# Sums on VectorE, whole quarter loads and a written order for three engines in two lead-ins of a decoder layer

## The chip, the cores and the metric

The kernel runs on one core of a Trainium2 chip. Its time is the device time of one execution in microseconds (us). The engines are named as in the profile: PE is TensorE (PEld its weight loads), DVE is VectorE, ACT is ScalarE, POOL is GpSimd, SP is SyncE, which issues the DMAs here.

## The reference

One decoder layer on 1024 tokens of width 1024, all in float32: token mixing (stick-breaking attention beside a state-space mixer), cross-attention to 256 memory tokens, and a SwiGLU feed-forward of hidden width 2816. Each of the three is normalised before and after and added to the stream.

```python
h = rms_norm(x, g_pre_mix[l])
...
x = x + rms_norm(merged @ w_mix_out[l], g_post_mix[l])
h = rms_norm(x, g_pre_xa[l])
mem_n = rms_norm(mem, g_mem[l])
x = x + rms_norm(memory_cross_attention(h, mem_n, w_xq[l], w_xkv[l], w_xo[l]), g_post_xa[l])
h = rms_norm(x, g_pre_ffn[l])
x = x + rms_norm(swiglu(h, w_gu[l], w_down[l]), g_post_ffn[l])
```

The two places that the change touches are `h @ w_xq`, the first product of the cross-attention, and the first four blocks of `h @ w_gu`, the first product of the feed-forward.

## The kernel before

A product of float32 matrices is made of three matmuls on the high and low parts of its operands: high by high, high by low, low by high. The high part of a weight is rounded by ScalarE (`hi_sb`, L98), the low part is the difference, made by VectorE or GpSimd (`lo_of`, L101). `acc3` (L216 to L223) makes one product of a 512-row weight block of 128 columns with 512 tokens, 12 matmuls of 128x512, into one PSUM bank.

The two projections go by a scheme of Strassen's kind on 2x2 blocks. The activation `h` has the blocks b11, b21, b22 and the combinations t1 to t4, each kept as a high and a low tile; of a weight come the quarters q11, q12, q21, q22, and from them s1 = q21 + q22, s2 = s1 - q11, s3 = q11 - q21, s4 = q12 - s2. Seven products make a pair of output rows (p = 0 and 1, since a quarter holds two column blocks).

A lead-in is the stretch in which such a projection begins while the output projection before it ends. `out_proj` (L1431 to L1458) works through the last four chunks of 128 tokens; each chunk is normalised (`pre_norm`, L159 to L172: ScalarE's square, two small GpSimd operations for the root, VectorE's scaling on L163), then transposed by TensorE and spread by `put` (L1497 to L1510: two copies on ScalarE, six 128x512 operations on VectorE). The list `late` holds the transposes and the put of the chunk that is still to be done. Products that need only the first half of the tokens (b11, b21) are made while the last chunks are on their way: `lead_products` makes three of them from weights that were split ahead; n0, n1 (of quarter n11), q1 (of q12) and n2, n3 (of n12) come next. n11, n12, n21, n22 are the quarters of the second pair of output rows. `first_sum` (L1577) adds two products: ScalarE copies the one out of PSUM (L1578), VectorE adds the other (L1579). `other_products` (L1581 to L1623) then does t1, t2, t3, b22 and t4 for one pair; it runs twice, the first time also splitting the blocks t2 to t4 (`other_blocks`). The sums s1 to s4 are made by GpSimd (`combined`, L1587).

The order of the products on TensorE is written out by hand: `in_turn` (L1563) holds each product behind the one before it. The other engines' order is the scheduler's, but for a few places held by `behind`. In the query projection the raw quarters q21, q22 and q12 lie in free halves of the result tiles `qT`, two halves of two tiles each (`parted`), so each is loaded by two DMAs of 256 KB; n11 and n12 lie whole in qT6 and qT7, and q11, n21, n22 in buffers of the pool `t4`. In PSUM the query lead-in has two single banks (`bank`) and two tiles of two banks each (`two_banks`); the feed-forward gives the pool of the two-bank tiles back after its first sums and opens `psf`, six single banks.

Of the kernel before, what the change touches and what calls it, by code (L numbers as in the profile page):

```python
# [16 lines left out]
P = 128  # L17
# [15 lines left out]

@with_exitstack
def hybrid_block(ctx, tc, a, out, dbg=None):
    nc = tc.nc
    V, A, G, T = nc.vector, nc.scalar, nc.gpsimd, nc.tensor
# [51 lines left out]
    def hi_sb(o, i, eng=None):  # L89
        if eng is None:  # L90
            turn[0] += 1
            eng = "pa"[turn[0] % 2]
        if eng == "p":
            return G.tensor_scalar(o, i, 1.0, 0.0, ALU.mult, ALU.add)  # L94
        elif eng == "v":
            return V.tensor_copy(o, i)
        else:
            return A.activation(o, i, AF.Copy)  # L98

    def lo_of(o, i, hi, eng=V):  # L100
        return eng.tensor_tensor(o, i, hi.bitcast(F32), ALU.subtract)  # L101
# [48 lines left out]
    rstd_ops = []  # L150

    def rstd_of(ms):
        r = mk(stats, [P, 1], F32, "rstd")
        G.tensor_scalar(r, ms, EPS, None, ALU.add)  # L154
        rstd_ops.append(G.tensor_tensor(r, r, mhalf, ALU.pow))
# [3 lines left out]
    def pre_norm(psp, xt, yt, gbc, put):  # L159
# [5 lines left out]
        def turns():  # L165
# [5 lines left out]
            put(pts, yt)  # L171
# [1262 lines left out]
    def out_proj(half, act, w, t4, psp, x_src, x_dst, gpost, gpre, put, ahead=None):  # L1434

        wh, wl = w
        for ci in range(4):
# [19 lines left out]
            if late:  # L1457
                late.pop()()  # L1458
# [68 lines left out]
    def quarter(t):  # L1527

        v = t.rearrange("p (k b f) -> p k b f", k=4, b=2)
        return [(v.rearrange("p k b f -> p k (b f)"), 0, 2 * P)], [v[:, :, p] for p in range(2)]  # L1530

    def parted(h0, h1):

        v = [h.rearrange("p (k f) -> p k f", k=4) for h in (h0, h1)]
        return [(x, p * P, P) for p, x in enumerate(v)], v

    def quarter_load(q, w, kh, c0):
        for dst, o, n in q[0]:
            ins = nc.sync.dma_start(dst, w[kh * 512:(kh + 1) * 512, c0 + o:c0 + o + n].rearrange("(k p) f -> p k f", p=P))
        return ins  # L1540

    split_ops = []

    def split_weight(pl, tag, x, eng=V):
        o = mk(pl, [P, 2, 4, P], F32R, tag)
        split_ops.append([hi_sb(o[:, 0], x, "a"), lo_of(o[:, 1], x, o[:, 0], eng)])
        return o[:, 0], o[:, 1]

    def lead_weights(wbig, w):
# [4 lines left out]
        ws = {(0, p): split_weight(ld, "sw", raws[0][:, :, p]) for p in range(2)}  # L1554
        o = mk(wbig, [P, 2, 4, P], F32R, "wraw", 2)
        hi_sb(o[:, 0], raws[1][:, :, 0], "a")
        lo_of(o[:, 1], raws[1][:, :, 0], o[:, 0])
        ws[1, 0] = o[:, 0], o[:, 1]
        return ws

    chain = []

    def in_turn(ps, w, b, first, last):  # L1563

        with behind(chain[-1:]):
            chain.append(acc3(ps, w, b, first, last))
        return chain[-1]

    def first_product(hb, w, nm, ps):
        return in_turn(ps, w, hb[nm], True, nm == "b21")  # L1570

    def lead_products(hb, ws, pa, pb0):
        first_product(hb, ws[0, 0], "b11", pa[0])
        first_product(hb, ws[0, 1], "b11", pa[1])
        first_product(hb, ws[1, 0], "b21", pb0)

    def first_sum(y, pa, pb):  # L1577
        A.activation(y, pa, AF.Copy)  # L1578
        V.tensor_tensor(y, y, pb, ALU.add)  # L1579

    def other_products(hb, pa, pc, q11, q12, q21, q22, sfp, swp, y, last, blocks=None):  # L1581

        a11, a12, a21, a22 = [q[1] for q in (q11, q12, q21, q22)]

        def combined(dst, x, z, op):
            for o, i, j in zip(dst, x, z):
                G.tensor_tensor(o, i, j, op)  # L1587
            return dst

        def rooms():  # L1590
            return [mk(sfp, [P, 4, P], F32, "sf") for _ in range(2)]
# [3 lines left out]

        def products(ps, ws, nm, start, stop, then):
            for p in range(2):
                in_turn(ps[p], ws[p], hb[nm], start, stop)
# [538 lines left out]
```

## Time and profile before

| | us |
|---|---|
| median of 3 runs | 2564.26 (2561.57 to 2564.91) |
| the profiled execution | 2562.7 |
| its span, first to last instruction | 2561.0 |
| PE busy | 2460.5 |
| DVE busy | 1818.6 |
| ACT busy | 1164.5 |
| POOL busy | 884.7 |

The mean granted TensorE clock is 0.992 of full speed. In the rows of the profile, "L1579" is the line of the kernel, "qT<-qT,p" says what is written from what, "x2" how many instructions the row holds, and the bracket at its end how long the engine was idle before it and what ended that. The query lead-in lies from about 1634 to 1735 us of the span, the one of the feed-forward from about 1897 to 1987.

### The profile page before, as it was taken

Reading aid. Unit: us, or ns where it says so; the run is one execution under the profiler, and the core shown is the slowest. Engines: PE = TensorE matmul, PEld = TensorE weight load, DVE = VectorE, ACT = ScalarE, POOL = GpSimd, SP = SyncE. Lnnn points to the kernel's source line nnn. Section 1 sums busy time; section 2 is a strip of 40 time slices with the busy share of each in tenths; the row PEclk is TensorE's granted clock in tenths of the full one; section 3 lists DMA queues with packets and bytes.
Section 4 is the critical chain, followed back from the end, with each engine's and each line's share of the span. In section 5 each row is a group of like instructions: output and inputs, shape, how many; then the busy total and the mean of one; then the engine's idle time right before and its main releaser. Section 6 shows DMA issues by size and latency. Waiting matters only on the chain. (4 is left out here: it accounts for less than half of the span.)

```text
span 2561.0 us, 33402 instructions
## 1 busy us (share of the span) xinstructions
PE 2460.5 (96%) x12306; PEld 2017.4 (79%) x12306; DVE 1818.6 (71%) x2131; ACT 1164.5 (45%) x2075; POOL 884.7 (35%) x672
## 2 busy tenths in 40 slices
PE   7999999999999999999999999889999999999998
PEld 5788888888788788777777778767777888888876
DVE  7765877766678787698898654745467566665997
ACT  5333555555566655566554203424334333334343
POOL 3221644443112111256665131311133233323662
PEclk9999999999999999999999999999999999999999
DMA  7441443333443443365342642401241222234232
GB/s 246 152 127 57 137 135 103 108 111 112 123 111 101 114 110 93 109 202 162 99 118 79 227 155 74 149 32 50 92 139 62 91 87 74 83 96 167 99 132 99
DMA packets 250718, 295.63 MB, mean 115 GB/s; under 512 B 17071, under 2 KB 170680, under 8 KB 250426
## 3 DMA queue, kind: packets, MB, share of 16 engines
q1 hardware_dynamic: 249978, 291.40, 36.4%
q8 instruction: 97, 1.59, 0.3%
q10 hardware_dynamic: 576, 2.10, 0.2%
q14 instruction: 67, 0.55, 0.1%
HBM read 202.20 MB, written 74.45 MB: 108 GB/s over the span
## 5 line engine op out<-in xcount | busy, mean ns | idle before, releaser
L903 DVE TENSOR_TENSOR_SCAN n<-n,mask 128x128 f32<-128x128 f32 (+7 forms) x128 | 187.7, 1491 | 24.6 <-ACT n L902 23.3
L101 DVE TENSOR_TENSOR sw<-sf,sw 128x512 fp32r<-128x512 f32 x166 | 137.3, 837 | 91.0 <-ACT sw L98 88.8
L98 ACT ACTIVATE sw<-sf 128x512 fp32r<-128x512 f32 x166 | 102.6, 627 | 136.3 <-PE mm L222 112.2
L920 ACT ACTIVATE wth<-tr,mone 128x512 fp32r<-128x512 f32 x192 | 110.6, 585 | 81.1 <-PE tr L917 79.1
L220 PE MATMUL mm<-h,sw 128*128 128x512 f32 x368 | 143.3, 389 | 2.6 <-ACT t L1615 2.6
L221 PE MATMUL mm<-h,sw 128*128 128x512 f32 x368 | 143.2, 389 | 0.0
L222 PE MATMUL mm<-h,sw 128*128 128x512 f32 x368 | 140.9, 389 | 0.0
L921 DVE SCALAR_TENSOR_TENSOR wtl<-tr,wth 128x512 fp32r<-128x512 f32 x192 | 99.5, 543 | 48.2 <-ACT wth L920 48.2
L101 DVE TENSOR_TENSOR sw<-wr,sw 128x512 fp32r<-128x512 f32 x113 | 107.1, 949 | 35.3 <-ACT sw L98 35.2
L98 ACT ACTIVATE sw<-wr 128x512 fp32r<-128x512 f32 x114 | 71.8, 630 | 111.6 <-PE mm L222 109.1
L188 POOL TENSOR_TENSOR sf<-wr,wr 128x512 f32<-128x512 f32 x36 | 51.0, 1416 | 205.3 <-DMA wr<-in_w_gu_dram 140.6
L685 DVE SCALAR_TENSOR_TENSOR b<-b,prmT,b 128x1023 f32<-128x1023 f32 (+2 forms) x72 | 109.5, 1521 | 16.9 <-ACT b L679 16.4
L94 POOL TENSOR_SCALAR v<-va 128x512 fp32r<-128x512 f32 x16 | 20.6, 1287 | 283.4 <-PE av L930 164.4
L154 POOL TENSOR_SCALAR rstd<-ms 128x1 f32<-128x1 f32 x74 | 29.4, 397 | 242.4 <-ACT x L1450 112.6
L902 ACT ACTIVATE n<-sc 128x512 f32<-128x512 f32 (+1 forms) x192 | 88.7, 494 | 46.7 <-PE tr L917 28.8
L104 PE MATMUL mm<-oth,bw 128*128 128x512 f32 x256 | 103.7, 405 | 3.2 <-DVE a L1242 3.2
L104 PE MATMUL p<-bw,h 128*128 128x512 f32 x256 | 99.6, 394 | 2.3 <-DVE x L1452 2.3
L106 PE MATMUL p<-bw,h 128*128 128x512 f32 x256 | 100.9, 395 | 0.5 <-DVE h L101 0.5
L105 PE MATMUL p<-bw,h 128*128 128x512 f32 x256 | 100.5, 393 | 0.0
L105 PE MATMUL mm<-otl,bw 128*128 128x512 f32 x256 | 100.5, 393 | 0.0
L106 PE MATMUL mm<-oth,bw 128*128 128x512 f32 x256 | 100.4, 392 | 0.0
L917 PE MATMUL tr<-ident,n 128*128 128x128 f32 x576 | 95.1, 274 | 3.3 <-DVE wtl L921 3.3
(678 smaller groups left out, 7993.7 us busy)
## 6 DMA issues: line engine op xcount, KB each, us to landing
wr<-in_w_in_dram SPq DMA_DIRECT2D x36, 512.0 KB
wr<-in_w_gu_dram SPq DMA_DIRECT2D x72, 256.0 KB
zr<-in_w_in_dram SPq DMA_DIRECT2D x28, 512.0 KB
wraw<-in_w_in_dram SPq DMA_DIRECT2D x20, 512.0 KB
gu_d<-t SPq DMA_DIRECT2D x36, 256.0 KB
zs_d<-zo SPq DMA_DIRECT2D x32, 256.0 KB
xs_d<-b SPq DMA_DIRECT2D x32, 256.0 KB
kl<-gt SPq DMA_DIRECT2D x64, 128.0 KB
```

The costliest lines, as they stand in the source:

```text
L98: return A.activation(o, i, AF.Copy)
L101: return eng.tensor_tensor(o, i, hi.bitcast(F32), ALU.subtract)
L104: first = T.matmul(ps, sh, mh, start=start, stop=False)
L105: T.matmul(ps, sh, ml, start=False, stop=False)
L106: T.matmul(ps, sl, mh, start=False, stop=stop)
L220: T.matmul(ps, w[0][:, k, :], bh, start=first and k == 0, stop=False, skip_group_check=True)
L221: T.matmul(ps, w[0][:, k, :], bl, start=False, stop=False, skip_group_check=True)
L222: ins = T.matmul(ps, w[1][:, k, :], bh, start=False, stop=last and k == 3, skip_group_check=True)
L685: V.scalar_tensor_tensor(acc[:, sh:], y[:, :S - sh], cw(3 - sh, f), acc[:, sh:], ALU.mult, ALU.add)
L903: V.tensor_tensor_scan(nt[:, 0:L][:, ::-1], nt[:, 0:L][:, ::-1], mask[:, S - L:][:, ::-1], 1.0, ALU.mult, ALU.max)
L920: A.activation(wh[:, t0 * P:], pt[:, t0 * P:], AF.Identity, bias=mone)
L921: V.scalar_tensor_tensor(wl[:, t0 * P:], pt[:, t0 * P:], -1.0, wh[:, t0 * P:].bitcast(F32), ALU.add, ALU.subtract)
```

## The change

It consists of five edits, all in the two lead-ins:

- The sums s1 to s4, and the low parts that GpSimd made, go to VectorE.
- A class `InTurn` wraps VectorE, ScalarE and TensorE. While it is on, each instruction is held behind the one before it on its engine, so that these three run in the order of the program. All instructions issued in that time carry the line L49.
- In the query projection the quarters n11, n12, q12 and q21 are loaded whole (512 KB each) into the middle of a pair of result tiles (`qP`, the right half of one with the left half of the next); q22 and q11 go to buffers of `t4`.
- Both lead-ins are now one function, `lead_in`, with one order of its steps (`stages`); the last chunk's transposes and its put are two steps that are placed apart.
- The feed-forward's lead-in works in the two-bank tiles too (`na`, `pb`), and opens `psf` behind it.

```diff
+class InTurn:
...
+    def __getattr__(self, name):
+        call = getattr(self.eng, name)
+        if not self.on:
+            return call
+
+        def run(*args, **kw):
+            with ExitStack() as st:
+                if self.last is not None:
+                    st.enter_context(self.tc.issue_after(self.last.ins))
+                self.last = call(*args, **kw)
+            return self.last
+        return run
...
-    V, A, G, T = nc.vector, nc.scalar, nc.gpsimd, nc.tensor
+    V, A, T = [InTurn(tc, e) for e in (nc.vector, nc.scalar, nc.tensor)]
+    G = nc.gpsimd
...
-            put(pts, yt)
+            return lambda: put(pts, yt)
...
+    def opening(hb, ws):
+
+        in_turn(True)
+        pa, pb = (bank(), bank()), two_banks()
+        acc3(pa[0], ws[0], hb["b11"], True, False)
+        acc3(pa[1], ws[1], hb["b11"], True, False)
+        late[0] = late[0]()
+        acc3(pb[0], ws[2], hb["b21"], True, True)
+        return pa, pb
...
         def combined(dst, x, z, op):
             for o, i, j in zip(dst, x, z):
-                G.tensor_tensor(o, i, j, op)
+                V.tensor_tensor(o, i, j, op)
             return dst
...
+        def stages(pa, pc, a11, a12, a21, a22, s1, s2, w1, w2, y, last, block, ahead):
+            products(pc, w1, "t1", True, False, lambda p: A.activation(y[p][1][1], pc[p], AF.Copy))
+            s3 = combined(a21, a11, a21, ALU.subtract)
+            w3 = weights(s3)
+            block("t3")
+            s4 = combined(room(), a12, s2, ALU.subtract)
+            products(pa, w2, "t2", False, False, lambda p: A.activation(y[p][0][1], pa[p], AF.Copy))
+            w4 = weights(s4)
+            products(pa, w3, "t3", False, False, lambda p: V.tensor_tensor(y[p][1][1], y[p][1][1], pa[p], ALU.add))
+            w7 = weights(a22)
+            block("t4")
+            products(pc, w4, "b22", False, True, lambda p: V.tensor_tensor(y[p][0][1], y[p][0][1], pc[p], ALU.add))
+            more = ahead()
+            products(pa, w7, "t4", False, True, lambda p: last(p, pa[p]))
+            return more
+
+        n0, n1 = weights(n11)
+        late[0]()
+        first_sum(y[0][0][0], pa[0], pb[0])
+        na = two_banks()
+        acc3(na[0], n0, hb["b11"], True, False)
+        put = late[1]()
+        late.clear()
+        q1 = split_weight(swp, "sw", q12[1])
+        put()
+        blocks = other_blocks(hb, xf, open_tx())
+        acc3(na[1], n1, hb["b11"], True, False)
+        acc3(pb[1], q1, hb["b21"], True, True)
+        n2, n3 = weights(n12)
+        first_sum(y[1][0][0], pa[1], pb[1])
+        acc3(pb[0], n2, hb["b21"], True, True)
+        s1 = combined(room(), q21, q22, ALU.add)
         w1 = weights(s1)
+        s2 = combined(room(), s1, q11, ALU.subtract)
+        first_sum(n00[0], na[0], pb[0])
+        acc3(pb[1], n3, hb["b21"], True, True)
         w2 = weights(s2)
+        first_sum(n00[1], na[1], pb[1])
+        blocks["t2"]()
+
+        def second():
+            s1 = combined(room(), n21, n22, ALU.add)
+            w1 = weights(s1)
+            s2 = combined(room(), s1, n11, ALU.subtract)
+            return s1, s2, w1, weights(s2)
+
+        n21, n22 = [pick(r()) for r in nq[2:]]
+        more = stages(pa, pb, q11, q12, q21, q22, s1, s2, w1, w2, y, last, lambda nm: blocks[nm](), second)
+        stages(na, pb, n11, n12, n21, n22, *more, ny(), nlast, lambda nm: None, lambda: None)
+        in_turn(False)
...
+            spare = [qP[i].rearrange("p b s -> p (b s)")[:, HALF:HALF + S] for i in (3, 2, 0, 1)]
+            n11, n12, q12, q21 = [load(r, kh, c0) for r, (kh, c0) in zip(spare, ((0, 4), (1, 4), (1, 0), (0, 2)))]
+            q22, q11 = more(1, 2), more(0, 0)
...
-        psx.close()
-        psf = pool(px, "psf", 6, PSUM)
...
+        psx.close()
+        psf = pool(px, "psf", 6, PSUM)
```

VectorE's order in the query lead-in, around the second `first_sum`. Before (in the names, `qT` are the result tiles, `p` a two-bank tile, `tr` the transposes, `sw` the split weights, `sf` the sums, `x` a buffer of `t4`, `xk` and `h` the blocks of the activation), from the norm to that sum:

```order
L163 SCALAR_TENSOR_TENSOR x_3127_15360<-wraw_15309,rstd_15389,g_pre_xa_14681 128x1024
L1579 TENSOR_TENSOR qT_3138_15438<-qT_3138_15438,p_3136_15396 128x512
L101 TENSOR_TENSOR sw_15466<-qT_3144_15444,sw_15466 128x512
L101 TENSOR_TENSOR sw_15469<-qT_3139_15439,sw_15469 128x512
L1503 TENSOR_TENSOR x_3127_15360<-tr_15484,xk_3048_14723 128x512
L101 TENSOR_TENSOR sw_15532<-qT_3145_15445,sw_15532 128x512
L101 TENSOR_TENSOR sw_15549<-qT_3145_15445,sw_15549 128x512
L101 TENSOR_TENSOR sw_15576<-sf_15572,sw_15576 128x512
L101 TENSOR_TENSOR sw_15579<-sf_15573,sw_15579 128x512
L1505 TENSOR_TENSOR h_3090_15043<-tr_15489,h_3089_15042 128x4x128
L1506 TENSOR_TENSOR xk_3050_14725<-tr_15489,x_3127_15360 128x4x128
```

Behind these stand three more of the put, one more low part, and then the sum into qT_3139. And now, from the end of the last put over that sum (into qT_3138) to the one behind it (into qT_3139):

```order
L49 TENSOR_TENSOR xk_3049_14724<-xk_3049_14724,xk_3050_14725 128x4x128
L49 TENSOR_TENSOR sw_15530<-qT_3139_15431,sw_15530 128x512
L49 TENSOR_TENSOR sw_15533<-qT_3139_15431,sw_15533 128x512
L49 TENSOR_TENSOR qT_3138_15430<-qT_3138_15430,p_3134_15378 128x512
L49 TENSOR_TENSOR sf_15550<-qT_3138_15430,x_3141_15446 128x512
L49 TENSOR_TENSOR sf_15551<-qT_3138_15430,x_3141_15446 128x512
L49 TENSOR_TENSOR sw_15554<-sf_15550,sw_15554 128x512
L49 TENSOR_TENSOR sw_15557<-sf_15551,sw_15557 128x512
L49 TENSOR_TENSOR sf_15560<-sf_15550,x_3142_15448 128x512
L49 TENSOR_TENSOR sf_15561<-sf_15551,x_3142_15448 128x512
L49 TENSOR_TENSOR qT_3139_15431<-qT_3139_15431,p_3134_15378 128x512
```

The whole put of the last chunk and the low parts of n12 now stand ahead of the second sum, the sums s1 and s2 (`sf`) stand on this engine between the second and the third, and the low parts of s1's weights come after the second sum instead of ahead of it.

ScalarE's order in the query stages, from the copies of the two t1 products on, now (`mm` are the single banks, `tx` the block t4):

```order
L49 ACTIVATE qT_3137_15429<-p_3134_15378 128x512
L49 ACTIVATE qT_3138_15430<-p_3134_15378 128x512
L49 ACTIVATE sw_15622<-qT_3138_15430 128x512
L49 ACTIVATE sw_15625<-qT_3138_15430 128x512
L49 ACTIVATE h_3151_15502<-xk_3048_14723 128x1024 x2
L49 ACTIVATE qT_3137_15429<-mm_15376 128x512
L49 ACTIVATE qT_3138_15430<-mm_15377 128x512
L49 ACTIVATE sw_15662<-sf_15632 128x512
```

Before, from the same copies on:

```order
L1612 ACTIVATE qT_3140_15440<-p_3136_15396 128x512
L98 ACTIVATE sw_15690<-sf_15586 128x512
L1612 ACTIVATE qT_3141_15441<-p_3136_15396 128x512
L98 ACTIVATE sw_15693<-sf_15587 128x512
L98 ACTIVATE tx_15570<-xk_3049_14724 128x1024 x2
L1615 ACTIVATE qT_3138_15438<-mm_15394 128x512
```

The high parts of s3's weights and of the block t3 (`h_3151`) now stand between the t1 copies and the t2 copies; before they were done ahead of the t1 copies, and the block t4 stood in their place.

More of the change, by code (lines that the diff above doesn't have):

```diff
@@ L1569, in first_product @@
[L1569 to L1583, printed above, removed]
+        return [split_weight(ld, "sw", raws[0][:, :, 0]), split_weight(ld, "sw", raws[0][:, :, 1]), split_weight(wbig, "wraw", raws[1][:, :, 0], 2)]
@@ L1696, in hybrid_block, with load @@
[L1696 to L1701 removed]
+            def load(q, kh, c0):
+                loads.append(quarter_load(q, w_xq, kh, c0 * P))
+                return quarter(q)
```

199 lines of the change are left out of this document (72 added, 127 removed).

## The prediction

> **What bounds the kernel now.** I read the page first (busy times, then the clock row), then the waits of TensorE in time, then a table of the stretches around the two lead-ins, last the rows of the engines that TensorE waits for there.
>
> ```profile
> span 2561.0 us, 33402 instructions
> ...
> PE 2460.5 (96%) x12306; PEld 2017.4 (79%) x12306; DVE 1818.6 (71%) x2131; ACT 1164.5 (45%) x2075; POOL 884.7 (35%) x672
> ```
>
> TensorE (PE) is busy for 96% of the span, so an edit that changes no matmul can only win idle time of TensorE (100 us in the whole program) or time in which its clock was lowered. The table of stretches shows how much of it lies in the two lead-ins. Its columns: stretch in us, its length, then the busy time of each engine (instructions), the granted TensorE clock, the DMA share, GB/s.
>
> ```profile
> core 0: us, PE busy (x) PEld busy (x) DVE busy (x) ACT busy (x) POOL busy (x), PEclk, DMA share, GB/s
> ...
> 1653.10:1660.85 7.75, 0.01 (x2) 0.03 (x1) 7.75 (x10) 3.84 (x5) 4.65 (x4) 0.83 0.18 53
> 1660.85:1665.80 4.95, 4.95 (x12) 3.61 (x12) 4.95 (x4) 0.69 (x1) 3.87 (x3) 0.57 0.66 229
> 1665.80:1669.84 4.04, 0.01 (x2) 0.03 (x1) 4.04 (x4) 0.63 (x1) 3.96 (x3) 0.83 0.32 136
> 1669.84:1676.16 6.32, 5.45 (x12) 3.78 (x13) 2.92 (x4) 0.63 (x1) 1.83 (x2) 0.57 0.26 83
> 1676.16:1735.27 59.11, 54.02 (x229) 42.49 (x230) 19.99 (x26) 16.44 (x27) 5.17 (x4) 1.00 0.03 10
> 1896.81:1911.85 15.04, 13.35 (x65) 10.42 (x63) 12.11 (x13) 7.90 (x15) 6.68 (x8) 1.00 0.49 173
> 1911.85:1916.37 4.52, 0.01 (x1) 0.04 (x1) 4.52 (x5) 1.66 (x3) 4.52 (x3) 0.77 0.00 0
> 1916.37:1921.15 4.78, 4.78 (x12) 3.78 (x12) 4.78 (x5) 2.01 (x3) 4.55 (x4) 0.51 0.01 3
> ...
> 1940.62:1943.22 2.60, 0.00 (x1) 0.00 (x1) 2.50 (x4) 1.69 (x4) 0.00 (x0) 1.00 0.00 0
> 1943.22:1987.06 43.84, 43.84 (x193) 36.31 (x194) 27.00 (x37) 15.45 (x26) 12.72 (x10) 1.00 0.22 74
> ```
>
> Query lead-in: TensorE stands for 7.75 and 4.04 us while VectorE (DVE) is busy all through, and after each wait its 12 matmuls take 4.95 and 5.45 us at a clock of 0.57. Feed-forward: waits of 1.69 (15.04 less 13.35), 4.52 and 2.60, and 12 matmuls in 4.78 at 0.51. What TensorE waits for, and the pace of its matmuls (start, duration, what ended the wait before):
>
> ```profile
> 1660.85 0.76 PE L220 MATMUL p<-a,sw 128*128 128x512 f32 x1 [7.74 <-DVE qT L1579]
> ...
> 1662.27 0.63 PE L220 MATMUL p<-a,sw 128*128 128x512 f32 x1
> 1662.69 0.63 PE L221 MATMUL p<-a,sw 128*128 128x512 f32 x1
> ...
> 1669.84 0.76 PE L220 MATMUL p<-a,sw 128*128 128x512 f32 x1 [4.03 <-DVE qT L1579]
> ...
> 1676.16 0.47 PE L220 MATMUL p<-h,sw 128*128 128x512 f32 x1 [0.87 <-ACT sw L98]
> ...
> 1676.94 0.39 PE L220 MATMUL p<-h,sw 128*128 128x512 f32 x1
> 1677.17 0.39 PE L221 MATMUL p<-h,sw 128*128 128x512 f32 x1
> ...
> 1679.86 0.50 PE L220 MATMUL p<-h,sw 128*128 128x512 f32 x1 [0.69 <-ACT qT L1612]
> ...
> 1697.25 0.50 PE L220 MATMUL p<-h,sw 128*128 128x512 f32 x1 [0.78 <-DVE qT L1620]
> ```
>
> The long waits are for the sums of L1579 on VectorE, which free the two-bank tile. A matmul starts every 0.43 us (1662.27 to 1662.69) at the lowered clock and every 0.23 (1676.94 to 1677.17) at the full one; a product of 12 takes about 2.8 us. Each reuse of the tile costs 0.69 (freed by ScalarE) or 0.78 (freed by VectorE). And why VectorE is late, GpSimd (POOL) first:
>
> ```profile
> 1644.11 3.98 POOL L1587 TENSOR_TENSOR sf<-qT,qT 128x512 f32<-128x512 f32 x2
> 1648.05 3.44 POOL L1587 TENSOR_TENSOR sf<-sf,x 128x512 f32<-128x512 f32 x2
> ```
> ```profile
> 1641.05 0.69 DVE L1508 TENSOR_TENSOR xk<-xk,xk 128x512 f32<-128x512 f32 x1
> 1641.66 0.68 DVE L1509 TENSOR_TENSOR xk<-xk,xk 128x512 f32<-128x512 f32 x1
> ...
> 1642.86 2.37 DVE L163 SCALAR_TENSOR_TENSOR x<-wraw,rstd,g_pre_xa 128x1024 f32<-128x1024 f32 x1
> ...
> 1649.16 2.88 DVE L101 TENSOR_TENSOR sw<-qT,sw 128x512 fp32r<-128x512 f32 x2
> 1651.96 3.44 DVE L101 TENSOR_TENSOR sw<-sf,sw 128x512 fp32r<-128x512 f32 x2
> ...
> 1660.03 0.67 DVE L1579 TENSOR_TENSOR qT<-qT,p 128x512 f32<-128x512 f32 x1
> 1660.63 2.35 DVE L101 TENSOR_TENSOR h<-xk,h 128x1024 fp32r<-128x1024 f32 x2
> ```
>
> Alone, one 128x512 operation follows the next after 0.61 us (1641.05 to 1641.66). While GpSimd runs a sum, two take 2.88 and 3.44, so 1.4 to 1.7 each. A 128x1024 costs 1.18 alone (2.35 for two).
>
> **The change, part by part.** *Sums to VectorE.* One low part and L1587 leave GpSimd, nearly all of the 19 us in the POOL column from 1653.10 on; nothing else waits for that engine there, so this alone saves nothing. VectorE takes the sums at 0.61 each instead of 1.72 and no longer runs its own at 1.4 to 1.7. *Three engines in program order.* VectorE's queue then reads: the norm of L163, n0 and n1 low, six of chunk 6's put, the first sum, q1 low, six of chunk 7's put, n2 and n3 low, the second first-sum. The norm cannot start before the GpSimd root that it waits for in any order, near 1642.1; put at 1.2 it ends at 1643.3. Behind it are 19 operations of 0.61: 1643.3 + 11.6 = 1654.9, and TensorE restarts about 0.15 later (1660.03 + 0.67 to 1660.85 now), at 1655.0.
>
> TensorE, which has no fewer products to do ahead of that point, arrives at 1652.95 (1660.85 less 7.74, less the 0.17 that it now lost to GpSimd's low part, roughly): a wait of 2.0 in place of 7.74. Its product ends at 1657.8. The next one needs the third first-sum, seven operations on: 1654.9 + 7 x 0.61 = 1659.2, so 1659.3, a wait of 1.5 in place of 4.03, and it ends at 1662.1. The fourth first-sum must follow that product, 0.67 and the hand-overs: the t1 product starts at 1662.9 (a wait like the 0.87 of now) instead of 1676.16. If the clock stays up, the lead-in is **13.3 us** ahead here: 5.7 + 2.5 of waits, 2.1 + 2.6 of half-rate matmuls, the rest rounding.
>
> *What is late next.* In the stages behind, before had put each weight split where the scheduler found room; now all stand in one written order. Four places cost more than the 0.69 or 0.78 of now; the prices of ScalarE's work in them:
>
> ```profile
> 1679.21 0.60 ACT L1612 ACTIVATE qT<-p 128x512 f32<-128x512 f32 x1 [3.16 <-PE p L222]
> 1679.70 0.62 ACT L98 ACTIVATE sw<-sf 128x512 fp32r<-128x512 f32 x1
> ...
> 1683.92 2.00 ACT L98 ACTIVATE tx<-xk 128x1024 fp32r<-128x1024 f32 x2
> ```
>
> (a) The copy of the first t2 product goes to the half row in which the raw quarter q12 now lies, so it must wait for s4, which reads it. t1's second product ends at about 1662.9 + 2.8 + 0.7 + 2.8 = 1669.2. Then ScalarE, in order: that product's copy 0.6, two high parts of w3 (0.5 each), the two 128x1024 of block t3 (2.0): 1672.8. VectorE's second 128x1024 follows the second high part, 1674.0, then s4 twice, 1675.2; the copy, 1675.9. Two t2 products from 1669.2 end at 1674.8; the t3 product waits for 1676, **1.2 to 1.7** where there was none. I take 1.7, since each hand-over between the engines adds 0.1 or more. (b) The b22 add stands behind w7's two low parts and block t4's two 128x1024: 0.7 + 1.2 + 2.35 = 4.3 after t3's last product, 1.4 to 1.5 more than the 2.8 that the product itself takes: **1.5** more than 0.78. (c) In the second stage the copy of t1's first product stands behind two high parts and two last copies on ScalarE, 2.2 us, of which about 1.0 passes beside the product: **1.3** more. (d) The second stage has (a) again for n12, but with no block between, so 0.6 + 0.6 for the two s4: **1.2**. Given back: **5.7**, bounds 0 (all covered, as VectorE is busy for only 20 us of the 59 now) and 8 (0.6 more at each).
>
> *The feed-forward.* Removed: 1.69 + 4.52 + 2.60, and 4.78 becomes 2.8: **10.8**. Added in front, by the same count: the norm as now, then 8 operations, first sum, q1, six, n2, n3, first sum:
>
> ```profile
> 1905.05 1.27 DVE L163 SCALAR_TENSOR_TENSOR x<-wraw,rstd,g_pre_ffn 128x1024 f32<-128x1024 f32 x1
> ```
>
> 1906.25 + 19 x 0.61 = 1917.9. TensorE has two more products before that point than now (n0 and n1, 5.5 us), so it comes to 1911.85 - 1.69 + 5.5 = 1915.7, with two short waits of 0.3 at 1916.3: 1.7 to 2.2. The next wait is 1.5 as above: **4.5** in all. Behind, two two-bank tiles are reused where six banks of a pool of their own were in turn. Now the stretch from 1943.22 has not a moment idle (43.84 of 43.84). The query's stages with the same tiles lost 59.11 - 54.02 = 5.09. So 5.1 at least, with (b) 6.6; with (c) and (d), and eight sums of the gated product in the queue, up to 10. I take **9.0**, near the top, as all that made (a) to (d) is here too. Net of the feed-forward: 4.5 + 9.0 - 10.8 = **+2.7**.
>
> *Whole quarter loads, no third pool.* Three loads in place of six halves on SP; both lead-ins wait for VectorE and ScalarE, not for a transfer, in every row above: 0, and at most one short wait. Between and behind the lead-ins the order of no engine changes: 0.
>
> Sum: -13.3 + 5.7 + 2.7 = **-4.9**. The profiled execution took 2562.7 (span 2561.0 and 1.7 around it): 2557.8. It lies 1.6 under the median 2564.26, so I forecast **2559.4**; with the bounds above (give-back 0 to 8, feed-forward -1.2 to +3.7), 2550 to 2563.
>
> **The clock.** A wait shorter than those of today can lower it too:
>
> ```profile
> 1821.98:1830.00 8.02, 5.67 (x19) 4.52 (x19) 3.79 (x3) 2.09 (x4) 1.58 (x4) 0.79 0.17 67
> ```
> ```profile
> 1824.33 0.50 PE L104 MATMUL p<-bw,h 128*128 128x512 f32 x1 [2.35 <-DVE x L1452]
> ...
> 1826.08 0.63 PE L104 MATMUL p<-bw,h 128*128 128x512 f32 x1
> 1826.50 0.63 PE L105 MATMUL p<-bw,h 128*128 128x512 f32 x1
> ```
>
> After this wait of 2.35 eight matmuls came at 0.43 instead of 0.23: 1.6 lost. After the 2.60 at 1940.62 the clock stayed 1.00. I add nothing to the sum, but this is the slower rival. The Trainium skill ("TensorE: Matmul & The Clock Gate", section "HAM oscillation — how this bites in real kernels") gives the rule that only idle gaps over about 3.4 us lower the clock; by it none of the new waits would, and the sum stands. The row at 1824.33 contradicts it for a 2.35 us wait, so I give it no weight. The same page's section "A second HAM failure mode: psum-queue depth-cycling" speaks against the change: short idles between groups that cycle through banks made the clock swing in another kernel; by it the rival below would hold.
>
> **Rivals.**
> 1. *The stages absorb the order* (0.22). The places (a) to (d) cost nothing and the feed-forward's stages only the 5.1 of reuse: -13.3 + (4.5 + 5.1 - 10.8) = -14.5, so 2549.8; half way to it, 2554.6. For it: VectorE is idle for two thirds of the query's stages. Against: the waits come from order, not from load.
> 2. *The clock falls after the 2 us waits* (0.20), slower. There are eight of 1.5 to 2.3: two in front and (a) to (d) in the query, two in front in the feed-forward. At 1.6 each, three give back all but 0.1; seven, 11.2, end at -4.9 + 11.2 = +6.3: 2570. It decides from the fourth on. For it: the row at 1824.33. Against: 1940.62.
> 3. *VectorE's step is longer in a written order* (0.13). Operations that follow a fresh wait stand 0.73 apart, not 0.61, if 0.12 of hand-over isn't hidden: 26 operations in each front, 2 x 26 x 0.12 = 6.2: +1.3, 2565.6, within 0.2%. For it: many follow a high part of ScalarE. Against: 1641.05 to 1641.66 depend on one another too.
>
> That the change doesn't do what it says has no chance worth a number: the instructions have moved as told.
>
> **How the numbers follow.** The forecast has 0.45, and its own range is 2554 to 2563. A measurement of this kernel tells about 0.2%, 5.1 us, from no change, so the forecast lies on that line: of its 0.45 I put 0.28 on faster and 0.17 on within. Rival 1 is faster (0.22). Rival 2 is slower for 0.16 and within for 0.04, rival 3 within for 0.08, slower for 0.05. Faster 0.50, same 0.29, slower 0.21. For 8 in 10: from 2551 (most of rival 1) to 2568 (most of rival 2).
>
> **What would show it.** Right: GpSimd has no sum in the lead-ins, VectorE's two 128x512 rows stand 0.61 apart, the 7.74 is near 2.0 and the 4.03 near 1.5, no row of 0.63 on TensorE behind them, and the t1 product starts 13 us earlier; then a new wait ahead of t3's product and one over 2 ahead of b22's second; the stretch behind 1943 is no longer full. Wrong: VectorE still at 1.4 or more, matmuls 0.43 apart behind the 2 us waits, or a wait released by a DMA.

## The result and the profile after

| | before | after |
|---|---|---|
| median of 12 runs, us | 2564.93 (2561.57 to 2569.37) | 2563.06 (2557.67 to 2567.30) |
| the profiled execution, us | 2562.7 | 2566.68 |
| its span, us | 2561.0 | 2565.0 |

The ratio of after to before is 0.9991, with a 95% interval from 0.9982 to 1.0001: 2 us faster, which the measurement can't tell from no change. The forecast was 2559.4, within a range of 2551 to 2568.

The profiled execution of after is 4 us longer than that of before, though its median is lower. So the changed stretches must be taken out of the trace and compared alone. This is the table of stretches, with the columns shown in the prediction. The stretches begin and end at the same instruction in both kernels: the first product of the lead-in, the first t1 product, and the first instruction behind the stages (in the query it is the attention's first matmul, which in both kernels runs ahead of the last t4 product). Before:

```profile
1634.37:1676.16 41.79, 28.98 (x113) 22.36 (x112) 36.34 (x35) 16.73 (x27) 26.56 (x18) 0.84 0.44 145
1676.16:1735.11 58.95, 53.86 (x229) 42.33 (x229) 19.99 (x26) 16.44 (x27) 5.17 (x4) 1.00 0.03 10
1896.81:1929.57 32.76, 26.55 (x113) 21.18 (x112) 29.83 (x29) 17.43 (x27) 19.94 (x16) 0.90 0.28 96
1929.57:1986.89 57.32, 54.72 (x241) 44.97 (x240) 40.55 (x50) 23.23 (x39) 20.36 (x14) 1.00 0.20 64
```

After:

```profile
1638.02:1667.53 29.51, 25.96 (x114) 20.46 (x112) 21.89 (x34) 13.56 (x23) 1.58 (x4) 0.94 0.35 114
1667.53:1732.48 64.95, 55.77 (x228) 43.42 (x229) 32.10 (x44) 19.00 (x31) 1.05 (x1) 0.97 0.15 49
1894.44:1923.67 29.23, 24.91 (x113) 19.17 (x111) 21.53 (x33) 13.63 (x23) 1.58 (x4) 1.00 0.25 88
1923.67:1988.70 65.03, 56.91 (x241) 44.54 (x242) 43.52 (x61) 26.73 (x43) 10.62 (x8) 1.00 0.19 61
```

There are four differences: the query's front (the stretch up to the first t1 product) is 12.3 us shorter (41.79 to 29.51), its stages 6.0 longer, the feed-forward's front 3.5 shorter, its stages 7.7 longer. Together **-2.1 us**, close to the 1.9 between the medians. GpSimd's column falls from 26.56 to 1.58 in the first stretch, and VectorE's from 36.34 to 21.89 although it now does the sums: it was slow, not loaded. What makes the profiled execution longer lies outside, 6.1 us in all: the query lead-in already began 3.65 us later (1638.02 against 1634.37), though both kernels are the same up to there, and the parts between and behind the lead-ins took 0.3 and 2.2 us more. In the traces of all the kernels run for this study it began anywhere from 1631.0 to 1638.4.

What TensorE waits for in after, in time. Since one line now stands for all, a row holds a whole product of 12 matmuls or two of them:

```profile
1658.17 4.61 PE L49 MATMUL p<-a,sw 128*128 128x512 f32 x12 [1.85 <-DVE qT L49]
1663.62 3.06 PE L49 MATMUL p<-a,sw 128*128 128x512 f32 x12 [0.85 <-DVE qT L49]
1667.53 3.03 PE L49 MATMUL p<-h,sw 128*128 128x512 f32 x12 [0.85 <-DVE qT L49]
1671.24 3.01 PE L49 MATMUL p<-h,sw 128*128 128x512 f32 x12 [0.69 <-ACT qT L49]
...
1681.23 5.74 PE L49 MATMUL mm<-h,sw 128*128 128x512 f32 x24 [1.53 <-ACT qT L49]
...
1691.91 4.58 PE L49 MATMUL p<-h,sw 128*128 128x512 f32 x12 [2.23 <-DVE qT L49]
...
1705.37 5.73 PE L49 MATMUL p<-h,sw 128*128 128x512 f32 x24 [0.69 <-ACT qT L49]
1712.81 3.03 PE L49 MATMUL p<-h,sw 128*128 128x512 f32 x12 [1.71 <-ACT qT L49]
```

The 7.74 became 1.85, and the 4.03 became 0.85 (the slow product ahead of it took up the rest); the new waits of 1.53, 2.23 and 1.71 stand in the stages. Two products, at 1658.17 and 1691.91, take 4.6 instead of 3.0: the lowered clock. In the feed-forward:

```profile
1915.37 3.01 PE L49 MATMUL p<-a,sw 128*128 128x512 f32 x12 [1.90 <-DVE t L49]
1919.77 3.06 PE L49 MATMUL p<-a,sw 128*128 128x512 f32 x12 [1.38 <-DVE sw L49]
1923.67 3.06 PE L49 MATMUL p<-h,sw 128*128 128x512 f32 x12 [0.85 <-DVE sw L49]
1927.42 3.01 PE L49 MATMUL p<-h,sw 128*128 128x512 f32 x12 [0.69 <-ACT t L49]
...
1946.26 2.99 PE L49 MATMUL p<-h,sw 128*128 128x512 f32 x12 [2.23 <-DVE t L49]
...
1958.64 5.78 PE L49 MATMUL p<-h,sw 128*128 128x512 f32 x24 [1.24 <-ACT t L49]
```

Behind these come 0.69, 0.75, 0.78 and twice 0.87, where before had none. VectorE's side of it:

```profile
1653.83 0.68 DVE L49 TENSOR_TENSOR xk<-tr,x 128x512 f32<-128x512 f32 x1
1654.42 0.68 DVE L49 TENSOR_TENSOR h<-x,h 128x512 fp32r<-128x512 f32 x1
1655.02 1.29 DVE L49 TENSOR_TENSOR xk<-xk,xk 128x512 f32<-128x512 f32 x2
1656.23 1.29 DVE L49 TENSOR_TENSOR sw<-qT,sw 128x512 fp32r<-128x512 f32 x2
1657.43 0.68 DVE L49 TENSOR_TENSOR qT<-qT,p 128x512 f32<-128x512 f32 x1
1658.03 1.28 DVE L49 TENSOR_TENSOR sf<-qT,x 128x512 f32<-128x512 f32 x2
```

Every operation starts 0.60 after the one before, the sums (`sf`) as well. The second first-sum at 1657.43 is the 19th behind the norm, and TensorE restarts 0.06 after its end.

### The profile page after: what moved, and what is told of

It is laid out like the page before. It is cut to its first block, busy times and chain, and to the rows that moved or that the text cites. A ratio compares the mean times of both kernels' runs of the same rounds, so it can differ in the third digit from the quotient of the medians.

```text
span 2565.0 us, 33376 instructions
## 1 busy us (share of the span) xinstructions
PE 2463.0 (96%) x12306; PEld 2015.3 (79%) x12306; DVE 1815.1 (71%) x2165; ACT 1162.9 (45%) x2075; POOL 827.8 (32%) x638
## 3 DMA queue, kind: packets, MB, share of 16 engines
q8 instruction: 97, 1.59, 0.3%
## 5 line engine op out<-in xcount | busy, mean ns | idle before, releaser
L122 DVE TENSOR_TENSOR sw<-sf,sw 128x512 fp32r<-128x512 f32 x142 | 112.9, 806 | 76.4 <-ACT sw L119 74.7
L119 ACT ACTIVATE sw<-sf 128x512 fp32r<-128x512 f32 x142 | 87.5, 627 | 116.9 <-PE mm L241 100.3
L239 PE MATMUL mm<-h,sw 128*128 128x512 f32 x288 | 112.0, 389 | 0.0
L240 PE MATMUL mm<-h,sw 128*128 128x512 f32 x288 | 112.0, 389 | 0.0
L241 PE MATMUL mm<-h,sw 128*128 128x512 f32 x288 | 109.8, 389 | 0.0
```

The source lines that it names most:

```text
L239: T.matmul(ps, w[0][:, k, :], bh, start=first and k == 0, stop=False, skip_group_check=True)
L240: T.matmul(ps, w[0][:, k, :], bl, start=False, stop=False, skip_group_check=True)
L241: ins = T.matmul(ps, w[1][:, k, :], bh, start=False, stop=last and k == 3, skip_group_check=True)
```

## The experiments

In every table "query" and "feed-forward" are the lengths of the two lead-ins in one trace each, less those of the kernel before: the query's from its first product to its last t4 product, the feed-forward's from its first product to the first instruction behind its stages. The ratio is the time against the kernel before, run beside it. In the expectations, e5, e7 and e8 are the kernels called "s4 early", "single banks" and "banks and s4" in the tables, and e9 is that of the last section, on the front.

### One lead-in at a time

The query lead-in of the change with the feed-forward of before (L1777 to L1849 left as they were but for one call):

```diff
-        lead_in(hw, xf, fa, fb, (q11, q12, q21, q22), ...
+        other_products(hw, fa, fe, q11, q12, q21, q22, ...
+        other_products(hw, fc, fe, n11, n12, n21, n22, ...
```

> The changed query lead-in beside the feed-forward lead-in of before. Theory (the two lead-ins add up, and the time gained in the query's is carried to the end): the traces of the two kernels put side by side give -6.9 us over the query lead-in, so 6.9 us faster than before, a ratio of 0.9973, and the feed-forward lead-in again with waits near 4.5 and 2.6. Rival (what is gained ahead is lost again behind, in stages that wait for something else): about -2 us like the whole change, ratio 0.9991 or more.

And the other way round:

```diff
-            lead_in(hx, xf, xa, xb, (q11, q12, q21, q22), ...
+            other_products(hx, xa, xb, q11, q12, q21, q22, ...
+            other_products(hx, xc, xb, n11, n12, n21, n22, ...
```

> The query lead-in of before beside the changed feed-forward lead-in. Theory: the side-by-side reading gives +2.3 us from the place where the feed-forward lead-in begins to the place where it ends, so 2.3 us slower than before, ratio 1.0009: waits of 1.69, 4.52 and 2.60 and 12 slow matmuls gone, nine waits of 0.7 to 2.3 in their place. Rival (the six-bank pool did not matter, the loss in the profile of the change was due to the earlier start): no change or up to 4 us faster.

| | query, us | feed-forward, us | ratio (95% interval) |
|---|---|---|---|
| the change | -6.3 | +4.2 | 0.9991 (0.9982 to 1.0001) |
| query only | -7.3 | +1.6 | 0.9976 (0.9966 to 0.9985) |
| feed-forward only | -0.3 | +4.3 | 1.0007 (0.9996 to 1.0019) |

The two lead-ins add up: -0.0024 and +0.0007 make -0.0017, inside the interval of the whole. The query's half is a gain of 6 us, clear of no change; the feed-forward's half is a loss in the trace, 4.3, whose time alone doesn't tell it from nothing. The first expectation's rival falls. So does the second's, the earlier start, by the trace: here the feed-forward lead-in begins at 1896.35, 1.9 us behind that of the change, and is as much longer. (The -6.9 and +2.3 of the two expectations were read off from where matmuls of like number stood in the two traces; between the same instructions it is -6.3 and +4.2.) In the query-only trace the unchanged feed-forward came out 1.6 longer: its third wait was 3.21 instead of 2.60, and the clock fell behind it. So much can one trace differ.

### The sums, and the order, each alone

The sums back on GpSimd, with the written order:

```diff
-                V.tensor_tensor(o, i, j, op)
+                G.tensor_tensor(o, i, j, op)
```

> The changed kernel with the sums s1 to s4 on GpSimd as before, all else kept, the order of the three engines too. Theory (sums beside VectorE's own work make both engines slow, 1.7 us each, and the written order makes VectorE wait for them): the wait ahead of the third first-sum grows by about 4 us in each lead-in and the waits for s4 by 2 to 3 each, in all 8 to 14 us slower than the change. Rival (the order is what helps, the engine of the sums does not matter): within 2 us of the change.

Only TensorE held in program order:

```diff
-        for e in (V, A, T):
-            e.on, e.last = on, None
+        T.on, T.last = on, None
```

> The changed kernel with only TensorE held in program order, VectorE and ScalarE ordered by the scheduler. Theory (the written order keeps the first sums ahead of the sums for later stages): VectorE now has 24 operations between the norm and the second first-sum instead of 19, so that wait grows by 3 us from 1.85, while the waits of 1.5 and 2.2 in the stages shrink: 0 to 4 us slower than the change. Rival (the written order is what costs the stages 5 us in the query and 9 in the feed-forward): 4 to 8 us faster than the change.

The kernel before with the sums and the GpSimd low parts on VectorE:

```diff
-                G.tensor_tensor(o, i, j, op)
+                V.tensor_tensor(o, i, j, op)
...
-... ((n11[1][0], G), (n11[1][1], V), (q12[1][1], V))]
+... ((n11[1][0], V), (n11[1][1], V), (q12[1][1], V))]
...
-... ((q12[1][1], G), (n11[1][0], V), (n11[1][1], V))]
+... ((q12[1][1], V), (n11[1][0], V), (n11[1][1], V))]
```

> The kernel before with the sums and the low parts that GpSimd made on VectorE, and nothing else. Theory (the two engines hold each other up): VectorE has 20 operations of 0.61 between the norm, which ends near 1644.1 in the time of the kernel before, and the second first-sum, so TensorE restarts near 1656.4 instead of 1660.85, a wait of about 3.3 in place of 7.74; in the feed-forward the 4.52 falls as well: 4 to 9 us faster than before. Rival (the engine does not matter without the written order, since the scheduler now puts the sums ahead of the first-sums): no change, or slower by up to 5 us, like the kernel that leaves VectorE and ScalarE to the scheduler.

| | query, us | feed-forward, us | ratio (95% interval) |
|---|---|---|---|
| the change, sums on GpSimd | -3.9 | +8.1 | 1.0006 (0.9996 to 1.0017) |
| the change, only TensorE in order | +1.8 | +13.8 | 1.0066 (1.0051 to 1.0082) |
| before, sums on VectorE | -3.5 | -3.4 | 0.9974 (0.9964 to 0.9984) |

With the sums on GpSimd, VectorE is slow again. VectorE of that kernel:

```profile
1650.88 0.67 DVE L49 TENSOR_TENSOR xk<-tr,x 128x512 f32<-128x512 f32 x1
1651.47 1.18 DVE L49 TENSOR_TENSOR h<-x,h 128x512 fp32r<-128x512 f32 x1
1652.58 3.43 DVE L49 TENSOR_TENSOR xk<-xk,xk 128x512 f32<-128x512 f32 x2
```

and GpSimd in the same microseconds:

```profile
1652.05 1.73 POOL L1594 TENSOR_TENSOR qT<-x,qT 128x512 f32<-128x512 f32 x1
1653.74 1.71 POOL L1594 TENSOR_TENSOR sf<-sf,x 128x512 f32<-128x512 f32 x1
```

The mechanism is that of the prediction: 0.60 alone, 1.7 beside a sum, for an operation whose two inputs lie in SBUF. The row at 1650.88, which reads the transposes (`tr`) from PSUM, takes its 0.6 although GpSimd is in a sum from 1650.80 to 1652.11. (So do two such rows of the kernel before, at 1655.33 and 1655.93, beside GpSimd's sums from 1654.82 to 1657.75.) The size was not as expected: 6.3 us slower than the change in the two lead-ins (2.4 + 3.9), not 8 to 14, and in time the two intervals overlap. The first wait grew from 1.85 to 6.22:

```profile
1658.93 5.49 PE L49 MATMUL p<-a,sw 128*128 128x512 f32 x12 [6.22 <-DVE qT L49]
```

But the waits of 1.53 and 1.71 for s4 were gone, since GpSimd had made s4 by 1662.5, ahead of the t1 products.

Without the order on VectorE and ScalarE the change becomes the slowest kernel of all, far beyond the 4 us that I expected. What TensorE waits for there:

```profile
1663.88 4.44 PE L49 MATMUL p<-a,sw 128*128 128x512 f32 x12 [3.17 <-DVE qT L1601]
1674.30 5.05 PE L49 MATMUL p<-a,sw 128*128 128x512 f32 x12 [5.99 <-DVE qT L1601]
```

The scheduler puts sums and whole blocks of 128x1024 ahead of the first-sums (four such operations from 1667.74 to 1672.36, 4.6 us, ahead of the sum at 1673.48), and each of these waits, like those of 3.27 and 4.29 in the feed-forward, brings the lowered clock (4.4 to 5.1 for a product). So the written order is worth some 19 us to this code. The kernel before, with the sums on VectorE and nothing written, came out as its theory has it: 6.9 us shorter in the two lead-ins, a first wait of 2.79 where 3.3 was expected. It seems to beat the change, 0.9974 against 0.9991, but the two were not run beside each other, their intervals still overlap (0.9982 to 0.9984), and the two lead-ins differ: it is 2.8 us longer than the change in the query and 7.6 shorter in the feed-forward. It keeps long waits in the front (2.79 and 4.78 in the query, 4.04 in the feed-forward) and has no new one in the stages. So in the query the sums gain 3.5 without the rest of the change, the rest 3.9 without the sums, and both together 6.3; in the feed-forward the sums gain and the rest loses more. What the stages give back has another cause than the sums.

### What the stages wait for

The sums s4 earlier:

```diff
+            s4 = combined(room(), a12, s2, ALU.subtract)
             w3 = weights(s3)
             block("t3")
-            s4 = combined(room(), a12, s2, ALU.subtract)
```

> The changed kernel with the two sums s4 ahead of the weights s3 and of block t3, so that the copy of the t2 product no longer waits for them behind the block. Theory (that copy overwrites the quarter that s4 reads): the wait of 1.53 ahead of t3's first product in the query goes, the 1.71 in its second stage falls to about 0.7; with 0.3 for each wait that goes, 2.5 to 3 us faster than the change; the feed-forward, whose quarter is not overwritten, stays. Rival (VectorE's queue as a whole is late): t3's products now wait for their own low parts instead, within 1 us of the change.

Block t4 and the last weights earlier:

```diff
             w4 = weights(s4)
+            w7 = weights(a22)
+            block("t4")
             products(pa, w3, "t3", ...
-            w7 = weights(a22)
-            block("t4")
             products(pc, w4, "b22", ...
```

> The changed kernel with the weights of the last product and block t4 ahead of the adds of the t3 products on VectorE. Theory (the b22 add stands behind them): the wait of 2.23 ahead of the second b22 product falls to 0.8 in both lead-ins, 2.9 us faster than the change, and up to 1.6 more where the lowered clock behind the 2.23 goes too. Rival (those weights' buffers come free only when the t2 products end, so VectorE stands still and the t3 adds come late): a new wait ahead of b22's first product, 0 to 3 us slower.

The t1 and b22 products in two tiles of one bank each:

```diff
-        more = stages(pa, pb, q11, ...
+        pc = [mk(psp, [P, 4, P], F32, "tr").rearrange("p k t -> p (k t)") for _ in range(2)]
+        more = stages(pa, pc, q11, ...
-        stages(na, pb, n11, ...
+        stages(na, pc, n11, ...
```

> The changed kernel with the t1 and b22 products of both lead-ins in two single-bank tiles (those of the transposes, free by then) in place of the two halves of the shared two-bank tile. Theory (a reader of one half holds the other): the waits ahead of t1's first and second, b22's second and the same two of the second stage go: 0.85 + 0.69 + 2.23 + 0.69 + 0.78 in the query and 0.85 + 0.69 + 2.23 + 1.24 + 0.87 in the feed-forward, with 0.3 for each of the ten 14 us, faster than the change by 10 to 15 us. Rival (VectorE and ScalarE are what is late, the tile only shows it): t4's products then wait for block t4 and w7, and 3 us or less is left.

Both of these edits, s4 and the banks, and the same once more:

> The two edits of e5 and e7 together. Theory: they add up, 12 to 18 us faster than the change, so 14 to 20 faster than before (ratio 0.9922 to 0.9945). Rival: with the banks apart VectorE is the bound, and the two together are no better than the single banks alone.

> The kernel of e8 once more beside e9, since its trace shows the query lead-in 2.7 us shorter than e7's and its times do not. If the trace is right, ratio to before 0.9917 to 0.993 and e9 below it; if s4's place costs elsewhere what it gains, 0.993 or more.

| | query, us | feed-forward, us | ratio (95% interval) |
|---|---|---|---|
| s4 early | -9.7 | +4.2 | 0.9979 (0.9969 to 0.9990) |
| t4 early | -9.6 | +4.8 | 0.9978 (0.9964 to 0.9993) |
| single banks | -16.3 | -2.1 | 0.9928 (0.9909 to 0.9946) |
| banks and s4 | -17.6 | -2.1 | 0.9932 (0.9909 to 0.9954) |
| banks and s4, again | -18.6 | -2.1 | 0.9921 (0.9907 to 0.9934) |

With s4 early the wait ahead of t3's products is gone, and the 1.71 is 0.69:

```profile
1688.79 3.01 PE L49 MATMUL p<-h,sw 128*128 128x512 f32 x12 [2.23 <-DVE qT L49]
1701.75 5.73 PE L49 MATMUL p<-h,sw 128*128 128x512 f32 x24 [1.43 <-ACT qT L49]
1708.17 3.01 PE L49 MATMUL p<-h,sw 128*128 128x512 f32 x12 [0.69 <-ACT qT L49]
```

but the second t1 product of the second stage now waits 1.43 instead of 0.69, since ScalarE's copy of the first is late in its place. And this trace has no lowered clock behind the 2.23 (3.01 for the product), which is half of its gain of 3.4 in the query. The feed-forward stays, as expected: there the copy overwrites nothing that s4 reads. Block t4 early shortens the 2.23 to 1.50 in the query and to 0.87 in the feed-forward, where it comes back later:

```profile
1687.88 3.01 PE L49 MATMUL p<-h,sw 128*128 128x512 f32 x12 [1.50 <-DVE qT L49]
...
1967.43 5.73 PE L49 MATMUL p<-h,sw 128*128 128x512 f32 x24 [2.81 <-DVE t L49]
```

In the feed-forward's second stage VectorE now makes the low parts of the last weights ahead of the add of the first t3 product, and beside them GpSimd makes sums for the next blocks:

```profile
1963.31 3.46 DVE L49 TENSOR_TENSOR sw<-wr,sw 128x512 fp32r<-128x512 f32 x2
```
```profile
1964.52 1.70 POOL L210 TENSOR_TENSOR sf<-wr,sf 128x512 f32<-128x512 f32 x1
```

The two take 3.46 instead of 1.29, and that add is late: 2.81 where there was 0.78. In the query's second stage, where GpSimd does nothing then, the wait stays 0.78. So the moved work brought the wait with it where the two engines met again. Of the 3.3 us that the query is shorter than in the change, 2.6 are the clock, which fell nowhere in that lead-in (1.0 in the front, 1.6 behind the 2.23), and only 0.7 the shorter wait. In time neither s4 nor t4 early is clear of the change.

The single banks remove them. TensorE in the query's first stage (its t1 and b22 products now write `tr`):

```profile
1663.54 5.60 PE L49 MATMUL tr<-h,sw 128*128 128x512 f32 x24
1668.98 5.60 PE L49 MATMUL mm<-h,sw 128*128 128x512 f32 x24
1674.42 1.02 PE L1752 MATMUL p<-xk,qT 128*128 128x256 f32 x4
1676.11 5.74 PE L49 MATMUL mm<-h,sw 128*128 128x512 f32 x24 [0.66 <-ACT qT L49]
1681.68 5.60 PE L49 MATMUL tr<-h,sw 128*128 128x512 f32 x24
1687.12 5.60 PE L49 MATMUL mm<-tx,sw 128*128 128x512 f32 x24
```

One wait of 0.66 is left where four stood (0.85, 0.69, 1.53, 2.23). It is what remains of the 1.53: the t3 products still start 1.53 us after the t2 products' end (1674.58 to 1676.11), but four matmuls of the attention (L1752) have moved into that gap. The other three are gone. The feed-forward falls from 4.2 above the kernel before to 2.1 below it. The two lead-ins are 16.3 us shorter than in the change, a little more than the 10 to 15 expected. VectorE and ScalarE do the same work: they were not too slow; a tile of two banks made one half wait for the reader of the other. The rival falls. That s4 adds to it is seen in the trace only (1.2 and 2.2 us); in time the first pair shows nothing of it, the second comes out lower, as the first branch of its expectation has it, and the intervals overlap. (Between the same instructions the 2.7 of that expectation is 1.2.) Of the 2.2 in the second trace, 1.0 is the clock, which did not fall in its front.

### The front

```diff
-                V.tensor_tensor(x11, x2, x11, ALU.subtract)
-                V.tensor_tensor(x21, x21, x2, ALU.subtract)
+                def rest():
+                    V.tensor_tensor(x11, x2, x11, ALU.subtract)
+                    V.tensor_tensor(x21, x21, x2, ALU.subtract)
+                return rest
...
         first_sum(y[1][0][0], pa[1], pb[1])
+        rest()
...
-        s2 = combined(room(), s1, q11, ALU.subtract)
         first_sum(n00[0], na[0], pb[0])
+        s2 = combined(room(), s1, q11, ALU.subtract)
```

> The kernel of e8 with VectorE's written order mended at the front: the last two operations of the last chunk's put stand behind the second first-sum, and the sums s2 behind the third. Theory (each operation ahead of a first-sum costs TensorE 0.6 there): the wait of 1.84 to 1.90 in both lead-ins falls to about 0.7, the next from 1.4 to 0.85, and in the query no lowered clock follows: 3.5 to 5 us faster than e8, ratio to before near 0.991. Rival (what is put off is missed later, by the split of block t2 or by w2): the waits move to the t2 products, within 1 us of e8.

The ratio is 0.9914 (0.9900 to 0.9928), the query -19.5, the feed-forward -3.2. TensorE there:

```profile
1655.83 3.02 PE L49 MATMUL p<-a,sw 128*128 128x512 f32 x12 [0.85 <-DVE qT L49]
1660.29 3.06 PE L49 MATMUL p<-a,sw 128*128 128x512 f32 x12 [1.44 <-DVE qT L49]
```

Two operations less ahead of the sum, 1.2 us, and the wait is 1.0 shorter. The next one stayed at 1.44. VectorE between the second first-sum, which starts at 1655.08, and the third, at 1659.55:

```profile
1655.69 1.28 DVE L49 TENSOR_TENSOR xk<-xk,xk 128x512 f32<-128x512 f32 x2
1656.89 1.29 DVE L49 TENSOR_TENSOR sf<-qT,x 128x512 f32<-128x512 f32 x2
1658.28 1.35 DVE L49 TENSOR_TENSOR sw<-sf,sw 128x512 fp32r<-128x512 f32 x2
```

Six operations stand there, as many as before this edit: the two of the put (`xk`) have taken the place of the two sums s2. So the edit could not shorten this wait, and whether s2 is what it waits for was not tried. Each lead-in is about 1.0 shorter than in the second run of the banks and s4, not 3.5 to 5 in all, and in time the two can't be told apart. It is the fastest kernel of the study, 2543.33 us (median) beside 2567.97 of the kernel before.

## Why the prediction was right, and where its sizes were off

**The bound, and what VectorE wins: right.** The wait forecast at 2.0 was 1.85, the restart stood where 19 operations of 0.6 put it, and the front of the query was 12.3 us ahead instead of 13.3. The missing 1.0 is the clock, which fell behind the 1.85 here; in the query-only trace it did not, the next wait was 1.45, near the 1.5 forecast, and the front was 13.3 us ahead (41.79 to 28.48).

**What is given back in the query: right as a sum, in part by luck.** 5.7 forecast, 6.0 measured. (a) 1.7 was 1.53, shown by moving s4. (b) 2.28 was 2.23. (d) 1.9 was 1.71. (c), 1.3 more ahead of the second t1 product of the second stage, did not come: that wait is 0.69. In its place the clock fell behind the 2.23, which cost 1.6 and which the sum put at nothing. That the sum fits is luck in so far as these two nearly cancel. The mechanism of (c) is there elsewhere: that wait is 1.43 with s4 early, where the clock stayed up, and 1.24 in the feed-forward of the change. The cause of (b) was only half named: block t4 ahead of the add makes it late, but the add matters only because the tile is shared.

**The feed-forward: the term that was mis-sized.** Forecast +2.7, measured +4.2. I added up idle time, 4.5 in the front and 9.0 behind; the brackets of after come to 12.4 (with one of 0.19 ahead of those shown), 1.1 less; by the columns above, 4.3 in the front and 8.1 behind. That the 9.0 came so near is luck too: I took it because all that made (a) to (d) would be there, but (a) and (d) are not, since nothing is overwritten that s4 reads; (b) came, part of (c), and the reuse of the tiles. What I left out is that a wait costs more than its bracket says. At 1667.53 a t1 product starts, the next at 1671.24 after 0.69: 3.71 less 12 times 0.227 (the step of a matmul at the full clock: 24 start in the 5.44 us from 1663.54 to 1668.98 of the single banks) and less 0.69 leaves 0.30. Twelve waits instead of four make 2.4 us: 12.4 - 8.8 + 2.4 - 1.9 (the half-rate product) = 4.1. In the query the number of waits hardly changed, so leaving this out cost nothing there. The total, -4.9 forecast, is -2.1 in the traces: 1.0 of the 2.8 is the front of the query, 0.3 its stages, 1.5 the feed-forward. The forecast of 2559.4 lay 3.7 us under the measured 2563.06, within its range; of the two sides of the line on which it lay, the likelier by the chances, faster (0.50), is not the one that came (no change, 0.29).

**The rivals.** The first, that the stages absorb the order, fell. The second, the lowered clock behind waits of 2 us, is true in part: it came behind two of the eight and made each product 1.6 longer, as the prediction said (the first cost only 1.0, since the next wait shrank), too little to turn the sign. The third, a step of 0.73 on VectorE, fell: it is 0.60 in the rows shown. Only where low parts follow fresh high parts of ScalarE is there a trace of it: the four operations from 1658.03 to 1660.68 take 2.65 instead of 2.40. No wait of TensorE in the lead-ins was put down to a DMA; the whole quarter loads changed nothing that these traces show, and were not tried alone.

**Where the gain went.** The kernel before with nothing but the sums and the GpSimd low parts moved gained 3.5 and 3.4 us in the two lead-ins. In the feed-forward the shared two-bank tiles cost 6.3 (94.3 us with them, 88.0 with single banks), which leaves about 1.3 for the rest of the new order: -3.4 + 6.3 + 1.3 = +4.2. That remainder was not taken apart. In the query, which had the shared tiles before, the rest of the change added 2.8 to the 3.5.

## What to carry to other kernels

Two engines that slow each other down can both look busy: compare the step of one operation alone and beside the other before deciding that either is full. When TensorE waits again and again for the reader of a tile, give its halves tiles of their own before reordering the readers: here it was worth more than the change it was tested on. Count a wait as its idle time and the 0.3 us that it cost here beyond it, and compare changed stretches between the same instructions of two traces, since the unchanged rest can differ by more than the change is worth.

## What the runs showed of the hardware

The same kernel, run twice, had the lowered clock behind a wait of 1.84 in one trace and not behind 1.85 in the other. TensorE's product behind that wait, of the banks and s4:

```profile
1658.50 4.62 PE L49 MATMUL p<-a,sw 128*128 128x512 f32 x12 [1.84 <-DVE qT L49]
```

and the same again:

```profile
1653.54 3.01 PE L49 MATMUL p<-a,sw 128*128 128x512 f32 x12 [1.85 <-DVE qT L49]
```

Behind waits of 1.84 to 1.90 the clock fell in four traces of the query (1.85 in the change, 1.84 with s4 early, 1.90 with single banks, 1.84 here) and stayed in three. Behind the waits of 1.90 to 1.94 in the feed-forward it stayed in seven traces; in the eighth, with the sums on GpSimd, a wait of 1.94 was followed by two matmuls, 0.29 more of waiting and then the lowered clock (10 matmuls in 4.14). So a wait of this length lowers the clock sometimes, and its length alone does not decide it. The Trainium skill ("TensorE: Matmul & The Clock Gate", section "HAM oscillation — how this bites in real kernels") has the limit at idle gaps of about 3.4 us; these rows show it below 2.

What differs is where the wait falls in time. Each trace keeps a record of the granted clock. In it the stretches of lowered clock in the lead-ins last 3.41 us or twice that, and within one trace they lie whole steps of 3.41 apart (in the change they begin at 1658.79 and 1692.93, ten steps). The table of stretches, in such steps, of the banks and s4 (the clock is the column behind GpSimd's):

```profile
1655.70:1659.11 3.41, 1.57 (x8) 0.97 (x7) 3.41 (x7) 0.16 (x2) 0.00 (x0) 1.00 0.50 154
1659.11:1662.53 3.42, 3.42 (x10) 2.64 (x9) 3.10 (x5) 2.46 (x5) 0.00 (x0) 0.50 0.00 0
```

and the same again, where the steps are counted from 1246.85, the last fall of the clock ahead of them:

```profile
1649.62:1653.03 3.41, 2.07 (x10) 1.37 (x8) 3.41 (x7) 1.26 (x3) 0.00 (x0) 1.00 0.37 128
1653.03:1656.44 3.41, 2.90 (x12) 2.18 (x12) 3.31 (x6) 1.75 (x3) 0.00 (x0) 1.00 0.08 26
```

In the first run the whole wait lies in one step, TensorE is busy for 1.57 of its 3.41 us, and the next step has the clock at 0.50. In the second the wait is spread over two steps, with 2.07 and 2.90 busy, and the clock stays. In the change it is 1.55 busy and a fall. No sharp limit follows: with s4 early a step with 1.59 busy was followed by the full clock (behind the 2.23). No run moved a wait within the steps on purpose.

A wait costs TensorE about 0.3 us beyond the idle time that the row shows, as worked out above.
